# Out-projections from three fp32r terms, row statistics by column half, and a diagonal matrix in place of a scaled copy

## The chip, the cores and the metric

One Trainium2 core runs the whole forward pass as one program. The metric is the time of one execution on the device in microseconds, lower is better; it is given as the median of several runs. The engines are TensorE (PE, matmuls into PSUM), VectorE (DVE), ScalarE (ACT), GpSimd (POOL) and SyncE (SP, whose queue issues nearly all weight transfers here). Each engine takes its instructions in the order of the program and waits for the others by semaphores.

## The reference, cut to what matters

The input is 256 tokens by 1024 columns (and a second stream of 256 context tokens). Three attention blocks follow each other, each closed by an out-projection, a residual and a mixture of experts:

```python
# phase A: one block with two streams; then layers l = 0 and l = 1
h   = rms_norm(x, g1) (modulated in phase A)
p   = h @ w_in                      # 1024 x IN_WIDTH
mix = concat of the heads' outputs  # 256 x 1024, 8 slots of 128 columns
x   = x + mix @ w_out               # 1024 x 1024, the out-projection
h2  = rms_norm(x, g2)
x   = x + moe(h2)                   # 32 experts in 4 groups, top 2, hidden 512
...
out = rms_norm(x, g_final)          # after phase A's and the last block's experts
```

All weights and values are float32, and `mix @ w_out` and the norms have to be as good as float32.

## The kernel before, in words

**Weights.** Weights stream from memory in units of 1 MB (128 partitions x 2048 floats) into a ring of slots, 23 that rotate and 14 lent out for work space early in the program. `S.take()` gives the next unit in the order of the program, `S.borrow()` takes a slot for a work buffer, and `S.release()` gives slots back; the SP queue issues the units strictly in that order, each as soon as its slot is free. So a slot that is released late delays every unit behind it.

**Precision.** A matmul can take fp32 or fp32r (a shortened fp32). Where the weights are split, each operand is written as hi + lo, with hi a copy to fp32r and lo the difference, and `mm3` (line 561) makes three fp32r matmuls: hi·hi, hi·lo and lo·hi. The in-projections do that already: ACT copies (L821, L1950), DVE or POOL subtracts (L822, L1954). The out-projections take plain fp32 (`out_mm`, L596): per 128 rows and 512 columns 8 matmuls of fp32, which the trace records as 2 instructions each.

**Attention slots.** `run_items` (L762) is a software pipeline written by hand: in slot s the scores of item s, the softmax of an earlier item, its transposes (L2160), their copies (`pT`, L2162), the value matmuls (L2125, L2129), and then a filler from a string. In layers 0 and 1 the twelve items are `MMSSMMSSMMMM`; for an M item the softmax is L2144 (DVE), L2148 (DVE), L2149 (ACT), L2153 and L2154 (DVE) and L2155 (POOL scales one of its parts). The fillers hold the out-projection: `o` opens it, `o2` does its first two slots of `mix`, and so on to `o8`, all for rows 0 to 127 and columns 0 to 511. Phase A has a string of its own, with L1339, L1347 to L1354, L1290 and L1293 as one slot's score, softmax, transposes and copy.

**Out-projection and routing.** `out_route` does the other groups of the out-projection, `group(0, 512)`, `group(1, 0)`, `group(1, 512)` and `group(1, 768)`, adds the residual, and chooses the experts (`choose`, L703 one of its DVE steps; `split`, L726 and L727). Then the gather (L1520) and the expert matmuls (L1704) start.

**Experts.** The expert matmuls are fed by 1 MB units. The last block's results are scattered to rows (L1762) and added to X (L1893, L1895).

**Statistics and norm.** After the experts, ACT squares the new rows (L1873) and sums them; `inv_root` takes the inverse root by row half `a`. In `normB` DVE writes a scaled copy of X (L1967), TensorE transposes it in 16 pieces of 128x128 (L1976), and ACT and DVE write it as hi and lo (L1980, L1982). Only then can the in-projection start (L2001). In layer 0, POOL scales X itself (L1970).

Of the kernel before, what the change touches and what calls it, by code (L numbers as in the profile page):

```python
# [10 lines left out]
F32 = mybir.dt.float32  # L11
# [13 lines left out]
FILL_B = ". v0 v1 . u0 . . u1 p0 f p1 f+o o2 o4+o5 o6"  # L25
# [3 lines left out]
FILL_A = "k0 . k1 . . q . r1 va+vb+m1 m1 . m6+r2+rel sl sb . o+o4 o6 o7 ."  # L29
# [343 lines left out]
def hybrid_kernel(ctx: ExitStack, tc: tile.TileContext, A, out, dbg=None):  # L373
# [211 lines left out]
    def out_begin(ps, mixT, order):  # L585
        O = K()
        O.mixT, O.order, O.n = mixT, order, 0
        O.us = [S.take() for _ in range(4)]
        O.w = [u.t.rearrange("p (f c) -> p f c", f=4) for u in O.us]
        O.po = bank(ps, "tr")  # L590
        return O
# [11 lines left out]
    def out_route(kind, O, E, finish, wr, brow, xT, tmp, spent):  # L603
# [129 lines left out]
        S.release(*O.us[0:2])  # L733
# [8 lines left out]
        S.release(*O.us[2:4])  # L742
# [36 lines left out]
    def first_phase():  # L779
        with ExitStack() as es:  # L780
# [446 lines left out]
            mixT = b2.t.rearrange("p (a d) -> p a d", a=8)  # L1227
            r = inv_rms(wg, p, 64, [128, 512], "_")
# [20 lines left out]
            def values(h, dT, vals, w, kind):  # L1249
                hp, odd = h // 2, h % 2  # L1250
                if kind == "n":
# [8 lines left out]
                    act.activation(mixT[:, 6 + hp], po[:, 0:256], AF.Copy)  # L1260
# [12 lines left out]
                def norm():  # L1273
                    pq = bank(ps, "tr")
                    pe.matmul(pq, lhsT=ones, rhs=sq, start=True, stop=True)
                    r = inv_rms(wd, pq, 128, [128, 512], "_")
                    later.append(lambda: dve.scalar_tensor_tensor(
                        mixT[:, 2 * hp:2 * hp + 2].rearrange("p a t -> p (a t)"), po, gs, r, op0=OP.mult, op1=OP.mult))
                later.append(norm)

# [114 lines left out]

            def start_out():
                hold.O = out_begin(ps, mixT, range(8))
# [14 lines left out]
            def last_b():  # L1412
                last[1]()
                S.release(*lent[:8])
# [3 lines left out]
            jobs.update({f"o{n}": lambda n=n: out_part(hold.O, n) for n in range(1, 9)})  # L1418
            jobs.update({f"m{n}": lambda n=n: [mod_unit(mod2) for _ in range(n)] for n in range(1, 9)})
# [15 lines left out]
            def finish(a, sl, po):  # L1435
# [4 lines left out]
                             ([], [b2]))  # L1440

    def moe_phase(kind, l, R, final=None):
# [7 lines left out]
        with ExitStack() as es:  # L1450
# [283 lines left out]

            def down(p, src):
                s = st[p]
                s.y = []
                for hf in range(2):
                    pd = mm()
                    for f in range(nf):  # L1740
                        pair_mm(pd, lambda a, b: s.hT[:, f, a:b], src.down(p, f, hf), f == 0, f == nf - 1)
                        if hf == 1 and f == nf // 2:
                            scat(p, [(0, 0), (1, 0)])
                    end = p == NL - 1 and hf == 1
                    yh = wk.tile([128, 512], F32R, name="P" if end else "yh")
                    yl = wk.tile([128, 512], F32R, name="xg" if end else "yl")
                    if kind == 1:
                        dve.scalar_tensor_tensor(pd, pd, s.gt, gmod[:, hf * 512:(hf + 1) * 512], op0=OP.mult,  # L1748
                                                 op1=OP.mult)
                        act.activation(yh, pd, AF.Copy)  # L1750
                        dve.tensor_sub(yl, pd, yh.bitcast(F32))
                    else:
                        act.activation(yh, pd, AF.Copy, scale=s.gt)  # L1753
                        dve.scalar_tensor_tensor(yl, pd, s.gt, yh.bitcast(F32), op0=OP.mult, op1=OP.subtract)  # L1754
                    s.y.append((yh, yl))
# [107 lines left out]
            vrt = [[[cons.tile([128, 1], F32, name=f"f{c}{a}{i}") for c in "vrt"] for i in range(nv)] for a in range(2)]  # L1863

            def stats():
                junk = {}

                def square(a, i, hf, on_act):
                    v, o = y[2 * a + hf] if i == 0 else blk(X.t, a, hf), ss[:, a, i, hf:hf + 1]
                    if on_act not in junk:  # L1870
                        junk[on_act] = mm()
                    if on_act:
                        act.activation(junk[on_act], v, AF.Square, scale=1.0 / 32, accum_out=o)  # L1873
                    else:
                        dve.scalar_tensor_tensor(junk[on_act], v, 1.0 / 1024, v, op0=OP.mult, op1=OP.mult, accum_out=o)

                def total(a):
                    for i in range(nv):
                        v = vrt[a][i][0]
                        if i == 0:  # L1880
                            dve.scalar_tensor_tensor(v, ss[:, a, 0, 0:1], EPS, ss[:, a, 0, 1:2], op0=OP.add, op1=OP.add)
                        else:
                            dve.tensor_add(v, ss[:, a, 1, 0:1], ss[:, a, 1, 1:2])
# [407 lines left out]
```

## Time and profile before

| | us |
|---|---|
| median of 3 runs | 1371.52 (1367.01 to 1372.51) |
| profiled execution, its own time | 1366.64 |
| its span in the trace | 1364.5 |
| PE busy / DVE / ACT / POOL | 1202.4 / 428.9 / 340.0 / 92.7 |
| mean granted clock of TensorE | 0.956 of full speed |

The span is what the trace covers; 2.1 us lie around it. A busy PE is not a PE at its peak. The profile's slices show the transfers at their full rate in the expert stages and at rest for part of each attention stage.

### The profile page before, as it was taken

What the parts mean: (1) busy time and instruction counts of PE and PEld (TensorE: products, weight loads), DVE (VectorE), ACT (ScalarE), POOL (GpSimd) and SP (SyncE); (2) the same over time, 40 slices, a digit from 0 to 9 for tenths busy, and PEclk for the clock granted to TensorE, in tenths of its full rate; (3) what the DMA queues carried; (4) which work ended last, traced back from release to release, by engine and by line L of the source; (5) the groups of instructions that cost most, each with busy time, mean ns of one, the idle gap of its engine ahead of it and who ended that gap; (6) DMA issues with size and microseconds to landing.
All of it is one profiled execution on the core that took longest, in us unless ns stands there. A gap on an engine that the chain in (4) does not pass through costs nothing. (4 is left out here: it accounts for less than half of the span.)

```text
span 1364.5 us, 18768 instructions
## 1 busy us (share of the span) xinstructions
PE 1202.4 (88%) x7278; PEld 649.5 (48%) x7278; DVE 428.9 (31%) x1022; ACT 340.0 (25%) x706; POOL 92.7 (7%) x79
## 2 busy tenths in 40 slices
PE   5999999999976799999769998999768999999775
PEld 3788765554221144443248664543216856444221
DVE  5456453342101021221155434221105535322102
ACT  4432343221000010110145521211014642212102
POOL 1344100000000000000012100000000210000000
PEclk9999998999989899999879998998898999999988
DMA  9644508959999999999993547999999365899995
GB/s 370 249 183 174 212 32 329 379 217 397 421 421 421 421 421 421 420 418 421 420 421 143 221 193 322 422 421 420 421 420 419 137 278 215 360 420 421 421 421 222
DMA packets 64537, 459.40 MB, mean 337 GB/s; under 512 B 7409, under 2 KB 7729, under 8 KB 9905
## 3 DMA queue, kind: packets, MB, share of 16 engines
q1 hardware_dynamic: 64432, 458.04, 82.0%
q8 instruction: 62, 1.02, 0.3%
q14 instruction: 43, 0.34, 0.1%
HBM read 466.40 MB, written 1.05 MB: 343 GB/s over the span
## 5 line engine op out<-in xcount | busy, mean ns | idle before, releaser
L1704 PE MATMUL up<-ring,xg 128*32 128x512 f32 (+2 forms) x2016 | 366.0, 629 | 52.9 <-DMA ring<-in_gu_dram 29.5
L1704 PEld LDWEIGHTS up<-ring,xg 128*32 128x32 f32 (+2 forms) x2016 | 103.6, 125 | 284.0 <-issue 180.5
L1704 PE MATMUL mm<-ring,hdT 128*32 128x512 f32 (+2 forms) x1008 | 194.3, 634 | 35.1 <-DMA ring<-in_dn_dram 23.8
L561 PE MATMUL ps<-ring,ring 128*128 128x256 f32 (+1 forms) x960 | 143.3, 307 | 1.2 <-POOL ring L896 0.5
L561 PEld LDWEIGHTS ps<-ring,ring 128*128 128x128 f32 x960 | 128.2, 192 | 20.4 <-issue 5.2
L1720 DVE TENSOR_TENSOR hd<-hd,up 128x256 f32<-128x256 f32 (+1 forms) x32 | 16.7, 521 | 352.1 <-ACT hd L1719 332.5
L1704 PEld LDWEIGHTS mm<-ring,hdT 128*32 128x32 f32 (+2 forms) x1008 | 52.2, 125 | 149.8 <-issue 99.2
L1719 ACT ACTIVATE hd<-up 128x256 f32<-128x256 f32 (+1 forms) x32 | 14.9, 465 | 364.9 <-PE up L1704 364.9
L1520 PEld LDWEIGHTS mm<-P,ring 128*128 128x128 f32 x512 | 66.2, 199 | 12.2 <-issue 8.8
L1520 PE MATMUL mm<-P,ring 128*128 128x256 f32 x512 | 70.4, 294 | 0.7 <-DVE xg L1530 0.3
L596 PE MATMUL mm<-ring,ring 128*128 128x512 f32 (+1 forms) x192 | 64.1, 487 | 0.0
L1754 DVE SCALAR_TENSOR_TENSOR yl<-mm,gt,yh 128x512 fp32r<-128x512 f32 x38 | 28.5, 751 | 113.2 <-ACT yh L1753 113.2
L1748 DVE SCALAR_TENSOR_TENSOR mm<-mm,gt,gmod 128x512 f32<-128x512 f32 x24 | 18.2, 759 | 111.3 <-PE mm L1704 111.3
L1753 ACT ACTIVATE yh<-mm,gt 128x512 fp32r<-128x512 f32 x38 | 26.1, 687 | 108.1 <-PE mm L1704 73.0
L1750 ACT ACTIVATE yh<-mm 128x512 fp32r<-128x512 f32 x23 | 13.7, 597 | 143.3 <-DVE mm L1748 143.3
L2001 PE MATMUL ps<-ring,ring 128*128 128x256 f32 x384 | 49.3, 290 | 0.0
L2001 PEld LDWEIGHTS ps<-ring,ring 128*128 128x128 f32 x384 | 48.2, 197 | 0.2
L596 PEld LDWEIGHTS mm<-ring,ring 128*128 128x128 f32 x192 | 35.8, 190 | 23.7 <-issue 21.5
L1970 POOL TENSOR_SCALAR ring<-ring,fr 128x1024 f32<-128x1024 f32 x2 | 5.7, 2848 | 421.5 <-DMA ring<-in_win_dram 421.5
L822 POOL TENSOR_TENSOR ring<-ring,ring 128x1024 fp32r<-128x1024 f32 x12 | 29.9, 2490 | 56.4 <-ACT ring L821 49.3
L1954 DVE TENSOR_TENSOR ring<-ring,ring 128x1024 fp32r<-128x1024 f32 x24 | 28.1, 1222 | 14.6 <-ACT ring L1950 14.6
L1762 PE MATMUL po<-yh,sm 128*128 128x512 f32 x61 | 30.6, 502 | 1.7 <-ACT yh L1750 1.0
(459 smaller groups left out, 1340.1 us busy)
## 6 DMA issues: line engine op xcount, KB each, us to landing
ring<-in_gu_dram SPq DMA_DIRECT2D x128, 1024.0 KB, 19.7
ring<-in_dn_dram SPq DMA_DIRECT2D x124, 1024.0 KB, 19.7
ring<-in_up_dram SPq DMA_DIRECT2D x120, 1024.0 KB, 19.5
ring<-in_wmod_dram SPq DMA_DIRECT2D x24, 1024.0 KB, 6.9
ring<-in_win_dram SPq DMA_DIRECT2D x24, 1024.0 KB, 11.4
ring<-in_wout_dram SPq DMA_DIRECT2D x12, 1024.0 KB, 18.3
ring<-in_c_dram SPq DMA_DIRECT2D x2, 896.0 KB, 14.2
ring<-in_wsm_dram SPq DMA_DIRECT2D x2, 784.0 KB, 14.9
```

Of the source, the lines that this page charges most:

```text
L561: pe.matmul(out, lhsT=a, rhs=b, start=first and i == 0, stop=last and i == 2, skip_group_check=True)
L596: pe.matmul(po, lhsT=O.mixT[:, s, a * 128:(a + 1) * 128], rhs=O.w[2 * c + s // 4][:, s % 4, sl.start - 512 * c:sl.stop - 512 * c], start=( ...
L822: (pool if q else dve).tensor_sub(lo[:, sl], u.t[:, sl], hi[:, sl].bitcast(F32))
L1520: pe.matmul(o, lhsT=xx[:, a, dt * 128:(dt + 1) * 128], rhs=P[:, a], start=(k == 0), stop=(k == 3))
L1704: pe.matmul(out[w * e:w * e + w], lhsT=x_of(w * e, w * e + w), rhs=wt, start=start, stop=stop)
L1720: dve.tensor_mul(hd, hd, pu[:, hid:uw])
L1748: dve.scalar_tensor_tensor(pd, pd, s.gt, gmod[:, hf * 512:(hf + 1) * 512], op0=OP.mult, op1=OP.mult)
L1753: act.activation(yh, pd, AF.Copy, scale=s.gt)
L1754: dve.scalar_tensor_tensor(yl, pd, s.gt, yh.bitcast(F32), op0=OP.mult, op1=OP.subtract)
L1762: pe.matmul(y[2 * a + hf], lhsT=s.sm[:, a * 128:(a + 1) * 128], rhs=s.y[hf][i], start=False, stop=True, skip_group_check=True)
L1954: dve.tensor_sub(lo[:, sl], u.t[:, sl], hi[:, sl])
L2001: pe.matmul(p[:, f * 256:(f + 1) * 256], lhsT=w[pw][:, dt, f * 128:(f + 1) * 128], rhs=hT[ph][:, dt], start=(i == 0 and f == 0 and dt == 0 ...
```

## The change

Three things are changed together.

First, the out-projection takes `mm3` in place of fp32. Four new fillers, `w0` to `w3`, one for each unit of `w_out`, copy the unit to hi on ACT in two halves (L590 of the changed kernel) and subtract the first half on DVE and the second on POOL (L591). `mix` is stored as hi and lo as well (ACT and DVE; in phase A partly POOL). The hi and lo parts hold eight slots where the four units were, and `mix` two where it held one; they take over six work slots that were released earlier (`hu`, `hl`, `sets`), and are released after `group(1, 0)` and `group(1, 768)`. `normB` reserves 6 slots where it reserved 5.

Second, the statistics after the experts go by column half instead of row half, with DVE's keep and ACT's square on different halves, one inverse root for all four values, and, in the last expert block, matmuls of the two column halves interleaved by pairs of units.

Third, `normB` writes no scaled copy: DVE makes two diagonal matrices (the identity times the row scales), and TensorE multiplies X's pieces by them in fp32, which transposes and scales at once. POOL's scaling of X stands behind them.

```diff
-FILL_B = ". v0 v1 . u0 . . u1 p0 f p1 f+o o2 o4+o5 o6"
+FILL_B = ". v0 v1 . u0 . . u1 p0+w0 f+w1 p1+w2 f+w3+o o2 o4+o5 o6"
-FILL_A = "k0 . k1 . . q . r1 va+vb+m1 m1 . m6+r2+rel sl sb . o+o4 o6 o7 ."
+FILL_A = "k0 . k1 . . q . r1 va+vb+m1 m1 . m6+r2+rel sl+w0 sb+w1 w2 w3+o+o4 o6 o7 ."
...
+    def out_weights(O, hi, lo=None):
+        u, i = S.take(), len(O.us)
+        lo = lo or S.borrow(F32R)
+        for q in range(2):
+            sl = slice(q * 1024, (q + 1) * 1024)
+            act.activation(hi.t[:, sl], u.t[:, sl], AF.Copy)
+            (pool if q else dve).tensor_sub(lo.t[:, sl], u.t[:, sl], hi.t[:, sl].bitcast(F32))
+        if i < 2:
+            S.reserve(1)
+        S.release(u)
+        O.us.append((hi, lo))
...
-            pe.matmul(po, lhsT=O.mixT[:, s, a * 128:(a + 1) * 128],
-                      rhs=O.w[2 * c + s // 4][:, s % 4, sl.start - 512 * c:sl.stop - 512 * c], start=(k == 0), stop=(k == 7))
+            mm3(po, lambda z: O.w[2 * c + s // 4][z][:, s % 4, sl.start - 512 * c:sl.stop - 512 * c],
+                lambda z: O.mix[z][:, s, a * 128:(a + 1) * 128], k == 0, k == 7, flip=True)
...
         group(1, 0, 512, 2)
-        S.release(*O.us[0:2])
+        S.release(*O.us[0], *O.us[1])
...
         group(1, 768, 256, 4)
-        S.release(*O.us[2:4])
+        S.release(*O.us[2], *O.us[3])
...
+            square(0, 0, 0, True)
+            keep(1, 0)
+            square(1, 0, 0, True)
+            keep(0, 0)
+            square(0, 0, 1, True)
+            keep(1, 1)
+            square(1, 0, 1, True)
+            keep(0, 1)
...
+            inv_root(wx, v, 2 * nv, "", (r, t))
...
-            S.reserve(5)
+            S.reserve(6)
...
-            for hf in range(2):
-                for a in range(2):
-                    dve.tensor_scalar(blk(xn, a, hf), blk(X.t, a, hf), R.vrt[a][-1][1], None, op0=OP.mult)
...
+            for a in range(2):
+                dve.tensor_scalar(dg[:, a], ident, R.vrt[a][-1], None, op0=OP.mult)
...
-                        pe.transpose(pt[:, i * 256 + a * 128:i * 256 + (a + 1) * 128],
-                                     xn[:, a, (2 * dp + i) * 128:(2 * dp + i + 1) * 128], ident)
+                        pe.matmul(pt[:, i * 256 + a * 128:i * 256 + (a + 1) * 128],
+                                  lhsT=X.t[:, a, (2 * dp + i) * 128:(2 * dp + i + 1) * 128], rhs=dg[:, a], start=True,
+                                  stop=True)
...
-            mu = S.borrow()
+            mixu = [S.borrow(F32R) for _ in range(2)]
...
+            def store(i, src, **kw):
+                act.activation(mix[0][:, i], src, AF.Copy, **kw)
...
+                    dve.tensor_sub(mix[1][:, i], src, mix[0][:, i].bitcast(F32))
...
-                    S.release(hu, hl, *sets[0], *sets[1])
...
+            jobs.update({f"w{n}": lambda n=n: out_weights(O, sets[n // 2][n % 2], (hu, hl)[n] if n < 2 else None) for n in range(4)})
```

How instructions move shows on two engines in the attention slots of layer 0. The first is GpSimd, from the set-up of the items to the routing; `e` are an item's exponentials, L2155 scales them, and L727 is the routing's split. Before:

```order
L2096 COPY wsm<-ring_1793 128x256
L2098 TENSOR_TENSOR wrk<-ring_1793,vecs 128x288
L2155 TENSOR_SCALAR e<-e,sm 128x128 x8
L727 TENSOR_TENSOR ring_6383<-ring_5615,ring_6382 128x1024
L1825 TENSOR_LOAD info
```

And the same place after, where L2155 is L2200 and L727 is L741:

```order
L2132 COPY wsm<-ring_2292 128x256
L2134 TENSOR_TENSOR wrk<-ring_2292,vecs 128x288
L2200 TENSOR_SCALAR e<-e,sm 128x128 x4
L591 TENSOR_TENSOR ring_2090<-ring_2179,ring_5712 128x1024
L591 TENSOR_TENSOR ring_5711<-ring_2181,ring_5713 128x1024
L2200 TENSOR_SCALAR e<-e,sm 128x128
L591 TENSOR_TENSOR ring_6392<-ring_112,ring_5714 128x1024
L2200 TENSOR_SCALAR e<-e,sm 128x128
L591 TENSOR_TENSOR ring_6422<-ring_72,ring_5715 128x1024
L2200 TENSOR_SCALAR e<-e,sm 128x128 x2
L741 TENSOR_TENSOR ring_6496<-ring_5697,ring_6495 128x1024
```

Two subtractions of 128x1024 now stand ahead of the ninth item's scaling (item 8, counting M and S items from 0), one ahead of item 9's and one ahead of item 10's.

The second is ScalarE in the same slots; L2149 are the exponentials of an item, two rows each, L2162 the copies `pT`, L2220 a copy for the filler `p0` or `p1`, and L2131 stores `mix`. Before:

```order
L2220 ACTIVATE dT<-tr 128x256
L2149 ACTIVATE e,sm<-e,nm 128x256
L2149 ACTIVATE e,sm<-e,nm 128x128
L2201 ACTIVATE zm<-zm 128x384
L2225 ACTIVATE ring_77<-tr,vecs 128x256
L2149 ACTIVATE e,sm<-e,nm 128x256
L2149 ACTIVATE e,sm<-e,nm 128x128
L2131 ACTIVATE ring_77<-po 128x256
L2162 ACTIVATE pT<-tr 128x384
L2220 ACTIVATE dT<-tr 128x256
L2149 ACTIVATE e,sm<-e,nm 128x256
```

After, with L2265 for L2220, L2194 for L2149, L2207 for L2162, L2246 for L2201 and L2152 for the stores:

```order
L2265 ACTIVATE dT<-tr 128x256
L590 ACTIVATE ring_5712<-ring_2179 128x1024 x2
L2194 ACTIVATE e,sm<-e,nm 128x256
L2194 ACTIVATE e,sm<-e,nm 128x128
L2246 ACTIVATE zm<-zm 128x384
L2152 ACTIVATE ring_6048<-tr,vecs 128x256
L590 ACTIVATE ring_5713<-ring_2181 128x1024 x2
L2194 ACTIVATE e,sm<-e,nm 128x256
L2194 ACTIVATE e,sm<-e,nm 128x128
L2152 ACTIVATE ring_6048<-po 128x256
L2207 ACTIVATE pT<-tr 128x384
L2265 ACTIVATE dT<-tr 128x256
```

Each `w` filler's two copies stand at the end of their slot, ahead of the next slot's exponentials; the third and the fourth stand behind a `pT`, which waits for GpSimd's scaling of an item.

## Rows read from the trace of the kernel before

**Rows 1.** The page's second part: transfer rate in 40 equal slices of the span.

```profile
GB/s 370 249 183 174 212 32 329 379 217 397 421 421 421 421 421 421 420 418 421 420 421 143 221 193 322 422 421 420 421 420 419 137 278 215 360 420 421 421 421 222
```

**Rows 2.** Windows of two stages: stretch, length, engines' busy times, clock, DMA share, GB/s.

```profile
721.00:790.00 69.00, 64.91 (x413) 50.98 (x412) 33.95 (x73) 38.53 (x92) 12.52 (x14) 1.00 0.48 190
...
840.00:1050.00 210.00, 181.70 (x1178) 79.80 (x1171) 48.72 (x101) 43.73 (x86) 0.00 (x0) 0.94 1.01 421
```

**Rows 3.** The chain that ended last, 830 to 1032: start, us, what.

```profile
1004.87 20.77 DMA ring<-in_dn_dram
1025.68 3.62 PE mm L1704 x26
```

**Rows 4.** Timeline, SP queue, 736 to 860: start, length, unit transfers issued.

```profile
813.53 21.84 SPq L332 DMA_DIRECT2D ring<-in_dn_dram  x8
840.35 9.55 SPq L332 DMA_DIRECT2D ring<-in_gu_dram  x8
```

**Rows 5.** Timeline, PE: layer 0's out-projection groups and the first gather.

```profile
789.28 7.03 PE L596 MATMUL mm<-ring,ring 128*128 128x512 f32 x16
...
809.88 3.62 PE L596 MATMUL mm<-ring,ring 128*128 128x256 f32 x16
...
823.86 6.34 PE L1520 MATMUL mm<-P,ring 128*128 128x256 f32 x32
```

**Rows 6.** Timeline, PE: runs of 24 fp32r matmuls (`mm3` of 8), two widths.

```profile
89.22 5.73 PE L561 MATMUL ps<-ring,ring 128*128 128x512 f32 x24
...
764.32 3.12 PE L561 MATMUL ps<-ring,ring 128*128 128x256 f32 x24
```

**Rows 7.** Line groups, splits of other weights: duration in ns min/median/max.

```profile
L821 ACT ACTIVATE ring<-ring x24: 1041/1048/1064, 24.4 to 184.6; 128x1024 fp32r<-128x1024 f32 x24
L822 DVE TENSOR_TENSOR ring<-ring,ring x12: 1214/1224/1730, 25.5 to 184.8; 128x1024 fp32r<-128x1024 f32 x12
L822 POOL TENSOR_TENSOR ring<-ring,ring x12: 2392/2420/2857, 26.4 to 185.8; 128x1024 fp32r<-128x1024 f32 x12
```

**Rows 8.** Timeline, layer 0's slots 8 to 11.

```profile
771.03 0.37 ACT L2220 ACTIVATE dT<-tr 128x256 f32<-128x256 f32 x1
...
773.66 0.66 POOL L2155 TENSOR_SCALAR e<-e,sm 128x128 f32<-128x128 f32 x1 [9.70 <-PE ps L2139]
...
779.87 0.66 POOL L2155 TENSOR_SCALAR e<-e,sm 128x128 f32<-128x128 f32 x1 [0.35 <-DVE sm L2153]
```

**Rows 9.** Timeline, layer 0's routing: a DVE and a POOL operation side by side.

```profile
818.94 2.34 POOL L727 TENSOR_TENSOR ring<-ring,ring 128x1024 fp32r<-128x1024 f32 x1 [38.41 <-DVE o L702]
818.96 2.37 DVE L703 TENSOR_TENSOR o<-o,rg 128x32 f32<-128x32 f32 x1
```

**Rows 10.** Timeline, phase A: DVE's first softmax step of two slots.

```profile
235.23 0.42 DVE L1347 TENSOR_TENSOR pe<-ps,ring 128x256 f32<-128x256 f32 x1 [1.51 <-PE ps L1339]
239.38 0.42 DVE L1347 TENSOR_TENSOR pe<-ps,ring 128x256 f32<-128x256 f32 x1 [2.00 <-PE tr L1290]
```

**Rows 11.** Timeline, from the last scatters of phase A's experts to layer 0's norm.

```profile
690.87 0.50 PE L1762 MATMUL po<-yh,sm 128*128 128x512 f32 x1
...
692.00 1.06 PE L1704 MATMUL mm<-ring,hdT 128*32 128x512 f32 x8
...
694.01 0.60 ACT L1750 ACTIVATE P<-mm 128x512 fp32r<-128x512 f32 x1 [4.13 <-DVE mm L1748]
...
696.74 0.58 ACT L1873 ACTIVATE mm<-po 128x512 f32<-128x512 f32 x1
...
703.40 1.66 DVE L1967 TENSOR_SCALAR ring<-ring,fr 128x512 f32<-128x512 f32 x4
...
704.03 3.77 PE L1976 MATMUL ps<-cm,ring 128*128 128x128 f32 x16 [7.48 <-DVE ring L1967]
```

**Rows 12.** A window there; columns as in Rows 2.

```profile
704.00:708.00 4.00, 3.97 (x18) 3.85 (x19) 2.89 (x8) 3.15 (x8) 3.05 (x2) 0.50 1.02 421
```

**Rows 13.** Timeline, PE: one fp32 matmul of 128x128, two records.

```profile
760.91 0.38 PE L2198 MATMUL tr<-sp,ones 128*128 128x128 f32 x2
```

More of the change, by code (lines that the diff above doesn't have):

```diff
@@ L583, in banks, with out_new, out_begin @@
         return E
-    def out_begin(ps, mixT, order):
+    def out_weights(O, hi, lo=None):
[9 more added lines that the diff above has]
+        O.us.append((hi, lo))
+        O.w.append([v.t.rearrange("p (f c) -> p f c", f=4) for v in (hi, lo)])
+    def out_new(mix, order):
         O = K()
-        O.mixT, O.order, O.n = mixT, order, 0
-        O.us = [S.take() for _ in range(4)]
-        O.w = [u.t.rearrange("p (f c) -> p f c", f=4) for u in O.us]
+        O.mix, O.order, O.n = mix, order, 0
+        O.us, O.w = [], []
+        return O
+    def out_begin(O, ps):
         O.po = bank(ps, "tr")
-        return O
     def out_mm(O, po, a, sl, ks):
@@ L1733, in tr, with split_y @@
                 dve.tensor_scalar(s.sm, iota, gt[:, p % 2, 0:1], None, op0=OP.is_equal)
+            def split_y(p, hf, pd):
+                s = st[p]
+                end = p == NL - 1 and hf == 1
+                yh = wk.tile([128, 512], F32R, name="P" if end else "yh")
+                yl = wk.tile([128, 512], F32R, name="xg" if end else "yl")
+                if kind == 1:
+                    dve.scalar_tensor_tensor(pd, pd, s.gt, gmod[:, hf * 512:(hf + 1) * 512], op0=OP.mult, op1=OP.mult)
+                    act.activation(yh, pd, AF.Copy)
+                    dve.tensor_sub(yl, pd, yh.bitcast(F32))
+                else:
+                    act.activation(yh, pd, AF.Copy, scale=s.gt)
+                    dve.scalar_tensor_tensor(yl, pd, s.gt, yh.bitcast(F32), op0=OP.mult, op1=OP.subtract)
+                s.y[hf] = (yh, yl)
@@ L1735, in down @@
             def down(p, src):
                 s = st[p]
-                s.y = []
-                for hf in range(2):
[L1739 to L1755, printed above, removed]
@@ new lines, in down @@
+                s.y, pds = {}, {}
+                last = p == NL - 1
+                m = 2 if last else nf
+                for z in range(0, nf, m):
+                    for hf in range(2):
+                        if z == 0:
+                            pds[hf] = mm()
+                        for f in range(z, z + m):
+                            pair_mm(pds[hf], lambda a, b: s.hT[:, f, a:b], src.down(p, f, hf), f == 0, f == nf - 1)
+                            if hf == 1 and f == (nf - 1 if last else nf // 2):
+                                scat(p, ALL[0:2])
+                        if z + m == nf:
+                            split_y(p, hf, pds[hf])
@@ L1907, in moe_phase, with square @@
-            stats()
+            v, r, t = (cons.tile([128, 2, nv], F32, name=f"f{c}{nv}") for c in "vrt")
+            junk = {}
+            def square(a, i, hf, on_act):
+                x, o = y[2 * a + hf] if i == 0 else blk(X.t, a, hf), ss[:, a, i, hf:hf + 1]
+                if on_act not in junk:
+                    junk[on_act] = mm()
+                if on_act:
+                    act.activation(junk[on_act], x, AF.Square, scale=1.0 / 32, accum_out=o)
+                else:
+                    dve.scalar_tensor_tensor(junk[on_act], x, 1.0 / 1024, x, op0=OP.mult, op1=OP.mult, accum_out=o)
@@ L1908, in moe_phase @@
+            dve.scalar_tensor_tensor(v[:, :, 0:1], ss[:, :, 0, 0:1], EPS, ss[:, :, 0, 1:2], op0=OP.add, op1=OP.add)
+            if nv == 2:
+                dve.tensor_add(v[:, :, 1:2], ss[:, :, 1, 0:1], ss[:, :, 1, 1:2])
+                dve.scalar_tensor_tensor(v[:, :, 1:2], v[:, :, 0:1], EPS, v[:, :, 1:2], op0=OP.mult, op1=OP.add)
+            inv_root(wx, v, 2 * nv, "", (r, t))
+            vrt = [[r[:, a, i:i + 1] for i in range(nv)] for a in range(2)]
             if final is not None:
@@ L1933, in second_phase @@
             mark("normB")
[L1934 removed]
+            dg = lu.t[:, 1024:1280].rearrange("p (a t) -> p a t", a=2)
             hold = Unit()
@@ L1984, in second_phase @@
             low()
+            if l == 0:
+                for a in range(2):
+                    pool.tensor_scalar(X.t[:, a], X.t[:, a], R.vrt[a][0], None, op0=OP.mult)
             mark("inprojB")
@@ L2130, in pv @@
                               start=False, stop=True)
-                act.activation(mixT[:, slot + hp], po[:, 0:256], AF.Copy)
+                store(slot + hp, po[:, 0:256])
             def mla_item(h):
```

100 lines of the change are left out of this document (44 added, 56 removed).

## The prediction

> **What bounds the kernel now.** I read the transfer rates first [rows 1]. From slice 10 on the expert stages run at 418 to 422 GB/s, and the two attention stages between them fall to between 137 and 360. A 1 MB unit at 421 GB/s takes 2.49 us. The window of layer 0's experts shows the transfers busy all the time (share 1.01) and TensorE 181.7 of 210 us, while the window of its attention slots shows them 0.48 busy [rows 2]. The chain agrees: at the end of the experts it runs through the landings of the last units, and then a few matmuls [rows 3]. So an expert stage ends when its units have come, and an attention stage when its own chain of small steps has. What starts the stream again is the expert stage's first matmuls: the ring is full by then, SP's last eight issues before it are spread over 21.84 us, and the next eight come at 840.35, once slots come free [rows 4]. Therefore a shift of the end of the attention stage goes one to one into the end of the experts behind it, and so do slots that come free late. A gain on TensorE inside an expert stage would be worth nothing; a gain or a loss between the last landing and the first gather counts in full.
>
> **The out-projection groups.** A group of 512 columns takes 7.03 us in 16 records of fp32, one of 256 columns 3.62 [rows 5]. The same eight steps as 24 fp32r matmuls take 5.73 and 3.12 [rows 6]. So two groups save 1.30 and two 0.50: 3.6 us behind the slots, and 1.3 more for the group that is done inside the slots, which counts only if TensorE is what the slots wait for.
>
> **The weight splits.** The trace has the same splits for other weights: 1.05 us for an ACT copy of half a unit, 1.22 for DVE's subtraction, 2.42 for POOL's [rows 7]. One out-projection adds 8, 4 and 4 of these: 8.4, 4.9 and 9.7 us. The engines have room for them by sum, since DVE was busy 33.95, ACT 38.53 and POOL 12.52 of 69 us [rows 2]. But the slots are chains, and the order shows where the splits stand in them: two POOL subtractions ahead of item 8's scaling, one ahead of item 9's and one ahead of item 10's; and on ACT each pair of copies ahead of the next exponentials, the third and fourth pair behind a `pT` that waits for such a scaling.
>
> I follow layer 0 on the clock of before [rows 8]. `dT` ends at 771.40, the copies of `w0` at 773.5, DVE's part at about 774.6 (behind a step of its own), POOL's at 777.0. DVE's next step on the S item reads two buffers, and if it has to wait for POOL, the next exponentials come at 779.6 and end the copies of `w1` at 782.6; POOL is done at 785.0 and scales item 8 by 785.7. Before, that was done at 774.3. From there each slot is a ring of steps: transposes, `pT` and one more ACT store, about 1.45 together (three steps of the size of `dT`'s 0.37, with 0.1 each to hand over), two copies 2.1, POOL's subtraction 2.4, the scaling 0.66, in all 6.6 us. That gives 792.3 and 798.9 for items 9 and 10, and 799.6 for item 11, where 780.5 was before. From there to the end of the group in the slots it was 8.8 us (789.28); I take 6.2, since fewer of its matmuls are left and they are cheaper. The slots then end at about 806, 16.5 later.
>
> Whether DVE waits for POOL is the main unknown. In the routing a DVE step of 128x32 took 2.37 us, next to a POOL step of 2.34 that began 0.02 earlier [rows 9]; a subtraction of 128x1024 takes DVE only 1.22 [rows 7]. I read that as a lock on operations with two buffers as input. Without the lock the slots end 2.4 us earlier, at +14. The page SBUF — State Buffer of the Trainium skill (section on the two physically separate sides) states such a lock: VectorE and GpSimd share a pair of ports, and whichever starts first holds it for its whole instruction. By that rule the slots come out at +16.5, and without it at +14; the trace's 2.37 us agrees with the rule.
>
> I take +16, less 3.6 for the groups: +12.4 at the first gather (823.86 before [rows 5]). The ring adds a little: ten slots come free only with the groups, four behind `group(1, 0)` and six behind `group(1, 768)`, where five did before. Five more units at 2.49 us are 12.5 us of transfers which lay in idle time before and now start after about 825; the stream goes on without a gap from there, and its first units of the second round land 13 us later than before. I take 12.5 per layer, bounds +8 (ACT's copies find half their place in waits) and +16 (no overlap at all): **+25 for both layers**.
>
> **Phase A.** Its slots have the same four fillers, with two full sections of DVE and ACT ahead of the softmax: 1.05 + 1.22 = 2.27 us each, 9.1 for four. DVE's first softmax step waited 1.51 and 2.00 us for TensorE in two of the slots [rows 10]; so 3.5 are hidden and 5.6 remain, less 3.6 for the groups: **+2**. Bounds: -5 if all is hidden, +5.5 if nothing is.
>
> **Statistics and norm.** In phase A's last block the scatter of four matmuls stands ahead of the last eight matmuls (690.87 to 692.00, then 1.06 us), and now stands behind them; with the pairs interleaved, some 16 matmuls fewer are left behind the last landing. That brings `P` (694.01) forward by 1.1 + 1.5 = 2.6 us [rows 11]. Behind it the old way takes 9.4 us until 703.40; the new one has six squares on ACT of 0.58 and a read of the sum each [rows 11], overlapping the last scatter, and one root instead of two, so I expect the scale near 699.1 and TensorE's start near 699.5, 4.5 earlier than 704.03. Then it pays: the 16 transposes took 3.77 us, one record each, and an fp32 matmul of 128x128 is two records [rows 13]. At the clock that these transposes ran at, 0.50 of full speed [rows 12], the 1.2 GHz level, 16 more records cost 3.4 us; at 2.4 GHz the whole stage would be as long as it is now. I take half of that: **-3**, bounds -4.6 and -1. In layer 1 the statistics gain only 0.8, since nothing is interleaved there and only one root falls away, and the matmuls lose between 0 and 3.4: **+1**. The tail after the last experts has one root for two and no norm: 0.
>
> TensorE was idle for 7.48 us ahead of the transposes [rows 11], and the clock stayed at 0.50 for the first 4 us of transposes although TensorE was 3.97 of 4.00 us busy [rows 12]. The page TensorE: Matmul & The Clock Gate of the Trainium skill (Part 4, PE-mode transpose) says that the full clock does not engage for transposes. By that rule matmuls in their place could raise the clock early, and the two norms would be worth -4.5 and -1 in place of -3 and +1; no row here tells that from a clock that would have risen anyway.
>
> **The sum.** +25 + 2 - 3 + 1 = +25 on the profiled 1366.6, so **1391**; that execution is 4.9 us below the median of the runs shown, and I keep to it.
>
> **The rivals.** (1) *The splits are hidden* in the idle time of the three engines. Then each out-projection saves 4.9 us, three save 14.7, with 2 for the norms: about 1350. For it: the busy sums [rows 2]. Against it: four slots of such a chain have no more than a microsecond or two of slack each. It decides the sign where a split lengthens a slot by less than 0.9 us, since four slots times 0.9 are the 3.6 of the groups. (2) *Only ACT's copies count*, POOL's subtractions run beside the slots: four slots grow by 1.2 us, 4.8 less 3.6 is +1.2 per layer; with +1 in phase A and -2 in the norms, about 1368, no change. Against it: the scaling stands behind the subtraction in GpSimd's order. (3) *More is lost than the chain*: with long waits in the slots the clock falls to 1.2 GHz. It stood at 1.00 of full speed through the slots before [rows 2]; half speed through one group and the last slots costs 5 us per layer, and a gap of the same kind in phase A 3: about 1404.
>
> **How the numbers follow.** Forecast (1382 to 1398) 0.60; hidden 0.17; no change 0.10; more lost 0.13. A measurement of this kernel can tell about 0.5%, 7 us, from no change, so faster 0.17, same 0.10, slower 0.73. The range goes from 1363, below the no-change case, to 1404; it leaves out most of the hidden case and the end of the third.
>
> **What would show it.** In the changed profile: the four scalings of items 8 to 11 end near 786, 792, 799 and 800 on before's clock (slots of about 6.6 us); the out-projection groups at 5.7 and 3.1 us; DVE steps with two buffers as input stretched to POOL's end; the first gather 12 us later in each layer, counted from the end of the phase before; the norm's first matmul about 4.5 us earlier in layer 0; transfers at 421 GB/s to the end of each expert stage. The forecast is wrong if the slots stay near 4 us, if POOL's 2.4 us lie behind something longer, or if the late start of the experts is caught up because their units had already landed.

## The result, and the profile after

The changed kernel takes 1410.72 us (median, 1409.86 to 1410.94) where the kernel before takes 1369.26 (1366.26 to 1372.51) on the same chip: the ratio is 1.0308, with a 95% interval from 1.029 to 1.0326. The profiled execution has a span of 1408.2 us, 43.7 more than before. So the sign was as forecast, and the loss was 41 us where 25 were forecast, outside the range.

First the page's slices of the transfer rate, which answer to [rows 1]:

```profile
GB/s 368 256 175 203 151 31 269 327 355 422 421 421 421 421 421 421 421 420 421 419 232 90 80 292 421 421 421 421 421 419 276 91 78 298 419 421 420 421 421 226
```

The expert stages still run at 419 to 422; the valleys of the two layers are deeper, 80 and 78 where 143 and 137 were the lowest. Where the time went is read from stage to stage. This table has the start of certain instructions on TensorE's timeline of both kernels: the first gather of each expert stage, the last scatter, the first score of a layer.

| | before | after | shift | grown by |
|---|---|---|---|---|
| first gather, phase A | 285.71 | 288.90 | +3.2 | +3.2 |
| first score, layer 0 | 742.62 | 742.10 | -0.5 | -3.7 |
| first gather, layer 0 | 823.86 | 844.05 | +20.2 | **+20.7** |
| last scatter, layer 0 | 1031.43 | 1052.14 | +20.7 | +0.5 |
| first score, layer 1 | 1074.58 | 1096.12 | +21.5 | +0.8 |
| first gather, layer 1 | 1155.28 | 1195.47 | +40.2 | **+18.7** |
| last scatter, layer 1 | 1354.82 | 1398.81 | +44.0 | +3.8 |

Nearly all of it lies in the two layers' attention slots. The out-projection groups behind them did what was worked out: the timeline of TensorE, for [rows 5], has

```profile
813.37 5.62 PE L561 MATMUL mm<-ring,ring 128*128 128x512 f32 x24
...
830.52 3.12 PE L561 MATMUL mm<-ring,ring 128*128 128x256 f32 x24
...
844.05 6.13 PE L1556 MATMUL mm<-P,ring 128*128 128x256 f32 x32
```

5.62 and 3.12 us for 7.03 and 3.62. The splits cost what their rows said too; the line groups (duration in ns, minimum, median, maximum) for [rows 7]:

```profile
L590 ACT ACTIVATE ring<-ring x24: 1042/1046/1054, 233.0 to 1152.5; 128x1024 fp32r<-128x1024 f32 x24
...
L591 DVE TENSOR_TENSOR ring<-ring,ring x12: 1224/1225/1226, 234.1 to 1152.7; 128x1024 fp32r<-128x1024 f32 x12
L591 POOL TENSOR_TENSOR ring<-ring,ring x12: 2374/2431/2471, 235.1 to 1153.7; 128x1024 fp32r<-128x1024 f32 x12
```

What the slots did with them is in the timeline of layer 0 (start, us, engine, line, tiles; in brackets the idle time before and who ended it), from GpSimd's part of the first split on, with one row from ahead of it. L2237 is a step of an S item with two buffers as input, L2194 are the exponentials, L2199 and L2200 the scaling on VectorE and GpSimd, L2189 and L2193 the next item's first softmax steps:

```profile
764.98 0.35 DVE L2199 TENSOR_SCALAR e<-e,sm 128x256 f32<-128x256 f32 x1
...
777.68 2.43 POOL L591 TENSOR_TENSOR ring<-ring,ring 128x1024 fp32r<-128x1024 f32 x1 [11.87 <-ACT ring L590]
777.83 2.69 DVE L2237 SCALAR_TENSOR_TENSOR sp<-zm,sp 128x384 f32<-128x384 f32 x1
...
781.54 0.51 ACT L2194 ACTIVATE e<-e,nm 128x256 f32<-128x256 f32 x1 [3.94 <-DVE nm L2193]
...
784.12 1.99 ACT L590 ACTIVATE ring<-ring 128x1024 fp32r<-128x1024 f32 x2
...
785.20 1.22 DVE L591 TENSOR_TENSOR ring<-ring,ring 128x1024 fp32r<-128x1024 f32 x1 [0.46 <-ACT ring L590]
786.19 2.43 POOL L591 TENSOR_TENSOR ring<-ring,ring 128x1024 fp32r<-128x1024 f32 x1 [6.08 <-ACT ring L590]
...
786.54 2.24 DVE L2199 TENSOR_SCALAR e<-e,sm 128x256 f32<-128x256 f32 x1
788.61 0.64 POOL L2200 TENSOR_SCALAR e<-e,sm 128x128 f32<-128x128 f32 x1
788.70 0.54 DVE L2189 TENSOR_TENSOR e<-ps,ring 128x384 f32<-128x384 f32 x1
789.27 0.61 DVE L2193 TENSOR_REDUCE nm<-e 128x1 f32<-128x256 f32 x2
...
789.79 0.51 ACT L2194 ACTIVATE e<-e,nm 128x256 f32<-128x256 f32 x1 [3.67 <-DVE nm L2193]
...
797.75 0.51 ACT L2194 ACTIVATE e<-e,nm 128x256 f32<-128x256 f32 x1 [3.75 <-DVE nm L2193]
```

The reader is to see a ring. ACT copies, then DVE and POOL subtract, then DVE scales (2.24 us, where the same step alone takes 0.35, the first row), then DVE starts the next item's softmax, and only then ACT has its exponentials and can go on to the next copies. Only pieces of this overlap: DVE's subtraction runs beside the second copy, and DVE's scaling beside POOL's subtraction, with which it ends (788.78 and 788.62). The next item's softmax and exponentials run beside none of it. In the kernel before, these are the exponentials of the same slots:

```profile
769.39 0.51 ACT L2149 ACTIVATE e<-e,nm 128x256 f32<-128x256 f32 x1 [2.12 <-DVE nm L2148]
...
772.84 0.51 ACT L2149 ACTIVATE e<-e,nm 128x256 f32<-128x256 f32 x1 [1.44 <-DVE nm L2148]
...
774.87 0.51 ACT L2149 ACTIVATE e<-e,nm 128x256 f32<-128x256 f32 x1 [0.28 <-DVE nm L2148]
...
778.50 0.51 ACT L2149 ACTIVATE e<-e,nm 128x256 f32<-128x256 f32 x1 [1.63 <-DVE nm L2148]
```

They come 2.0 to 3.6 us apart; in the changed kernel 8.25 and 7.96.

### The profile page after: what moved, and what is told of

Read it like the earlier page. It is cut to its first block, busy times and chain, and to the rows that moved or that the text cites. A ratio compares the mean times of both kernels' runs of the same rounds, so it can differ in the third digit from the quotient of the medians.

```text
span 1408.2 us, 19149 instructions
## 1 busy us (share of the span) xinstructions
PE 1211.5 (86%) x7430; PEld 677.7 (48%) x7430; DVE 463.8 (33%) x1031; ACT 363.4 (26%) x723; POOL 126.6 (9%) x94
## 2 busy tenths in 40 slices
DMA packets 64540, 459.44 MB, mean 326 GB/s; under 512 B 7408, under 2 KB 7728, under 8 KB 9904
## 5 line engine op out<-in xcount | busy, mean ns | idle before, releaser
L1740 PE MATMUL up<-ring,xg 128*32 128x512 f32 (+2 forms) x2016 | 371.5, 640 | 54.8 <-DMA ring<-in_gu_dram 30.9
L561 PE MATMUL mm<-ring,ring 128*128 128x256 f32 (+1 forms) x288 | 52.8, 339 | 0.0
L561 PEld LDWEIGHTS mm<-ring,ring 128*128 128x128 f32 x288 | 44.4, 190 | 5.6
L836 POOL TENSOR_TENSOR ring<-ring,ring 128x1024 fp32r<-128x1024 f32 x12 | 29.9, 2494 | 56.3 <-ACT ring L835 49.3
L591 POOL TENSOR_TENSOR ring<-ring,ring 128x1024 fp32r<-128x1024 f32 x12 | 29.1, 2428 | 60.7 <-ACT ring L590 42.6
L2205 PE MATMUL tr<-cm,e 128*128 128x128 f32 x48 | 10.3, 333 | 27.4 <-POOL e L2200 27.4
```

Source lines behind the costliest of these rows:

```text
L561: pe.matmul(out, lhsT=a, rhs=b, start=first and i == 0, stop=last and i == 2, skip_group_check=True)
L591: (pool if q else dve).tensor_sub(lo.t[:, sl], u.t[:, sl], hi.t[:, sl].bitcast(F32))
L836: (pool if q else dve).tensor_sub(lo[:, sl], u.t[:, sl], hi[:, sl].bitcast(F32))
L1740: pe.matmul(out[w * e:w * e + w], lhsT=x_of(w * e, w * e + w), rhs=wt, start=start, stop=stop)
```

## The experiments

The distance from a layer's first score to its first gather is named *slots and groups* below; it is 81.2 and 80.7 us before (layers 0 and 1), 102.0 and 99.4 after. Each run was timed together with the kernel before. Where totals of two runs are compared, each is taken by its *loss*, its median less that of the kernel before beside it; the changed kernel's loss is 41.5 us.

**The parts alone.** `e1_norm_only` has the second and third part of the change and fp32 out-projections, `e2_proj_only` the first part alone, `e3_stats_only` the statistics and the interleaved last block alone. The edit of the third, seen from `e1_norm_only`:

```diff
-            for a in range(2):
-                dve.tensor_scalar(dg[:, a], ident, R.vrt[a][-1], None, op0=OP.mult)
+            for hf in range(2):
+                for a in range(2):
+                    dve.tensor_scalar(blk(xn, a, hf), blk(X.t, a, hf), R.vrt[a][-1], None, op0=OP.mult)
...
-                        pe.matmul(pt[:, ...], lhsT=X.t[:, a, ...], rhs=dg[:, a], start=True, stop=True)
+                        pe.transpose(pt[:, ...], xn[:, a, ...], ident)
```

> The kernel before with the second and third part of the change (statistics by column half, diagonal matrix) and the out-projections left as fp32. Theory (the loss is all in the attention slots of the out-projection's weight splits): faster than before by 2 to 4 us, from -3.8 in layer 0's norm and +1.1 in layer 1's, as the trace of the change has them, and -2.6 from the interleaved last block. Rival (the diagonal matrix or the statistics bring part of the loss): slower than before by 2 us or more.

> The kernel before with the first part alone: three-term out-projections with weight splits, and statistics and transposes as before. Theory: all of the loss and a little more, 1412 to 1416 us, with layer slots as long as in the changed kernel (24 us longer than before). Rival (the parts hurt each other, for example by the reserved slots or by the clock after the norm): clearly less, 1395 to 1405 us.

> The kernel before with the statistics by column half and the interleaved last block alone; the scaled copy and the transposes stay. Theory: faster than before by 4 to 6 us (4.5 in layer 0, 0.8 in layer 1), and so 1 to 3 us faster than the run with the diagonal matrix, since 16 more records on TensorE at half clock are not paid. Rival by the clock (real matmuls raise TensorE's clock, transposes do not): slower than the run with the diagonal matrix by 2 us.

Measured: 1365.94 us, ratio 0.9971 (0.9958 to 0.9983); 1416.23 us, ratio 1.0341 (1.0321 to 1.0361); and 1361.52 us, ratio 0.9946 (0.9929 to 0.9962), against 1369.45 of the kernel before. So the loss is the first part's, all of it, and the statistics alone are 7.9 us faster than the kernel before, more than the 4 to 6 expected. The diagonal matrix costs 4.4 us of that. In layer 0 the timelines of TensorE of the run with the diagonal matrix and of the one without show the stage itself:

```profile
698.85 5.74 PE L1972 MATMUL ps<-ring,ring 128*128 128x128 f32 x32 [5.54 <-DVE ring L1966]
```

```profile
698.50 3.77 PE L1976 MATMUL ps<-cm,ring 128*128 128x128 f32 x16 [5.74 <-DVE ring L1967]
```

32 records in 5.74 us for 16 in 3.77. The rival by the clock has something in it: these are windows of the two runs (stretch, length, busy times, granted clock, DMA), with the matmuls first,

```profile
700.00:702.00 2.00, 2.00 (x12) 2.00 (x11) 0.20 (x1) 0.84 (x2) 0.00 (x0) 0.50 1.01 422
702.00:704.00 2.00, 2.00 (x16) 2.00 (x16) 1.17 (x4) 1.04 (x3) 0.00 (x0) 0.77 1.02 413
704.00:706.00 2.00, 2.00 (x17) 1.77 (x16) 1.72 (x5) 2.00 (x5) 1.45 (x1) 1.00 1.00 418
```

and then the transposes:

```profile
700.00:702.00 2.00, 2.00 (x12) 2.00 (x10) 1.39 (x4) 1.91 (x6) 2.00 (x1) 0.50 1.03 430
702.00:704.00 2.00, 2.00 (x12) 2.00 (x11) 1.96 (x6) 2.00 (x5) 2.00 (x2) 0.50 0.99 406
704.00:706.00 2.00, 2.00 (x18) 2.00 (x18) 2.00 (x3) 1.03 (x2) 1.09 (x1) 0.95 1.04 431
```

With matmuls TensorE leaves its 1.2 GHz level about 1.3 us earlier: 0.77 and 0.95 are means of 0.50 and 1.00 over 2 us, which puts the rise at about 702.9 and 704.2. But that gains less than the 16 records cost: the in-projection starts at 704.35 in the one and at 701.92 in the other.

**The held ring slots.** `e7_hold` is the kernel before with the six work slots released behind the last group:

```diff
-                    S.release(hu, hl, *sets[0], *sets[1])
...
-            return out_route(2, hold.O, E, finish, wrk, brow[:, 1 + l], lu.t, lu.t, ([mu], [lu]))
+            return out_route(2, hold.O, E, finish, wrk, brow[:, 1 + l], lu.t, lu.t, ([mu, hu, hl, *sets[0], *sets[1]], [lu]))
```

> The kernel before, with the six work slots hu, hl and sets of layers 0 and 1 released only behind group(1, 768), as the change does, and nothing else. Theory (the held slots cost little as long as the slots' chain is what is late): the attention slots and the first gather stay as before, and the first units of the experts' second round land later, 0 to 14 us in all. Rival (the held slots are the main part of the loss): 25 us slower or more.

Measured: 1384.00 us, ratio 1.011 (1.0091 to 1.013), 14.5 us slower. The slots and groups stay as they were, 81.3 and 80.9. The time is lost behind them: from the first gather to the last scatter layer 0 takes 215.8 us for 207.6, layer 1 208.3 for 199.5. That is just above what the theory allowed (0 to 14), and not the main part of the loss. But the run holds more than the change does: it gives back two slots behind `group(1, 0)` and nine behind `group(1, 768)`; the changed kernel gives back four and six there, and the four raw units of `w_out` earlier, at the splits. So its 14.5 us are not the price of the change's held slots. In the changed kernel the same distances are 208.1 and 203.3, and in `e10_copies_only` below, which holds what the change holds, with slots and groups 1.5 and 5.0 us longer than before, they are 209.0 and 203.3: 1.5 and 3.7 us more than before.

**Which engine subtracts, and what stands behind it.** Three variants of the changed kernel. `e4_split_dve` has both subtractions on VectorE, `e5_scale_dve` moves L2200 from GpSimd to VectorE, `e6_store_late` writes the low part of each stored item of `mix` one slot later:

```diff
-            (pool if q else dve).tensor_sub(lo.t[:, sl], u.t[:, sl], hi.t[:, sl].bitcast(F32))
+            dve.tensor_sub(lo.t[:, sl], u.t[:, sl], hi.t[:, sl].bitcast(F32))
```

```diff
-                    pool.tensor_scalar(e[:, 256:384], e[:, 256:384], sm[:, 1:2], None, op0=OP.mult)
+                    dve.tensor_scalar(e[:, 256:384], e[:, 256:384], sm[:, 1:2], None, op0=OP.mult)
```

```diff
             def store(i, src, **kw):
+                settle()
                 act.activation(mix[0][:, i], src, AF.Copy, **kw)
...
-                    dve.tensor_sub(mix[1][:, i], src, mix[0][:, i].bitcast(F32))
+                    pend.append(lambda: dve.tensor_sub(mix[1][:, i], src, mix[0][:, i].bitcast(F32)))
...
```

`settle()` makes the subtractions that are pending.

> The changed kernel with both halves of each weight split's subtraction on VectorE, none on GpSimd. Theory (VectorE is held while GpSimd subtracts, and the scaling of the items stands behind it; VectorE then needs 1.22 us where it waited 2.4): each of the four slots shorter by 0.9 to 1.5 us, 4 to 6 us per layer, 1399 to 1404 us in all. Rival (VectorE becomes the bound, or the slots wait for ACT's copies alone): within 3 us of the changed kernel's 1410.7.

> The changed kernel with the third part of each M item's scaling moved from GpSimd to VectorE, so that nothing of the items stands behind a weight split in GpSimd's queue; the splits stay where they are. Theory by the lock (VectorE's own scaling waits for GpSimd's subtraction anyway): 0 to 4 us faster than the changed kernel. Rival by order (it is GpSimd's queue that makes the slots long): four times 2.4 us per layer, 15 to 20 us faster, 1391 to 1396 us.

> The changed kernel with the low part of each stored item of mix subtracted one slot later, so that VectorE's next reciprocal does not stand behind a subtraction that waits for ACT's store. Theory (this wait cost 3.9 us in layer 0 and 2.4 us in layer 1 ahead of the first split): 4 to 7 us faster than the changed kernel, 1404 to 1407 us. Rival (the splits' chain absorbs it): within 2 us.

Measured, against 1368.37 of the kernel before: 1412.63 us, 1.0325 (1.0304 to 1.0346); 1415.43 us, 1.0334 (1.0304 to 1.0365); 1407.32 us, 1.0287 (1.0267 to 1.0308). Slots and groups: 100.1 and 97.7; 103.3 and 100.9; 97.9 and 98.0. So GpSimd's queue is not the cause: with nothing of the items behind its subtractions the slots are no shorter (the rival by order falls). And with no subtraction on GpSimd at all, 1.8 and 1.6 us per layer come back, less than the 4 to 6 expected; phase A, where VectorE was busier, gave more than that away (its first gather at 294.42; runs with the changed kernel's own phase A have it from 288.63 to 291.26). VectorE's scaling takes 0.35 again, but the ring has the same order, with 2.36 us of subtraction on VectorE in it, and its turn is 7.5 us:

```profile
789.01 0.51 ACT L2194 ACTIVATE e<-e,nm 128x256 f32<-128x256 f32 x1 [2.93 <-DVE nm L2193]
...
792.67 2.36 DVE L591 TENSOR_TENSOR ring<-ring,ring 128x1024 fp32r<-128x1024 f32 x2 [0.46 <-ACT ring L590]
...
795.14 0.35 DVE L2199 TENSOR_SCALAR e<-e,sm 128x256 f32<-128x256 f32 x1
...
796.51 0.51 ACT L2194 ACTIVATE e<-e,nm 128x256 f32<-128x256 f32 x1 [2.92 <-DVE nm L2193]
```

The late store gave back 4.1 us in layer 0 and 1.3 in layer 1; its loss is 39.0 for 41.5, so 2.5 us in the whole, less than the 4 to 7 expected. In the changed kernel VectorE's reciprocal stood behind the subtraction of `mix`, which waited 1.97 us for ACT's store; TensorE then idled 2.35 us, and the next projection ran slower. First the changed kernel's timeline, then that of the late store:

```profile
764.45 0.42 DVE L2157 TENSOR_TENSOR ring<-po,ring 128x256 fp32r<-128x256 f32 x1 [1.97 <-ACT ring L2152]
764.79 0.15 DVE L2198 RECIPROCAL sm<-sm 128x2 f32<-128x2 f32 x1
...
765.86 0.55 PE L2205 MATMUL tr<-cm,e 128*128 128x128 f32 x3 [2.35 <-POOL e L2200]
766.17 4.60 PE L561 MATMUL ps<-ring,ring 128*128 128x256 f32 x24
```

```profile
764.55 3.11 PE L561 MATMUL ps<-ring,ring 128*128 128x256 f32 x24
```

**The subtractions left out.** `e9_copies_only` dropped them and let the third term read the high part of `w_out` with the high part of `mix`. That doubles the main term of the out-projection, and with it the values by which the experts are chosen.

> The changed kernel without the subtractions of the weight splits: only ACT's copies stay, and the matmuls of the low part read the high part in its place, so the output lacks the low part of w_out. Theory (of the 24 us that the slots grew by, GpSimd's subtractions and what waits for them are 2.4 to 2.7 us in each of four slots): 18 to 22 us faster than the changed kernel, 1389 to 1393 us; then the late release of the ring's slots, 14.5 us by itself, is the larger part of what is left. Rival (ACT's copies make the slots long): 8 us faster or less.

It took 1426.47 us, ratio 1.043 (1.0376 to 1.0483), with other transfers (446.89 MB for the changed kernel's 459.44), so its time says nothing on the slots. The slots and groups themselves, 82.9 and 85.9 us, agree with the next run. `e10_copies_only` has the third term read the high part of `w_out` with the low part of `mix`, which keeps the sizes:

```diff
-            (pool if q else dve).tensor_sub(lo.t[:, sl], u.t[:, sl], hi.t[:, sl].bitcast(F32))
...
+            for i, z in enumerate((0, 1, 1)):
+                pe.matmul(po, lhsT=O.mix[z][:, s, a * 128:(a + 1) * 128],
+                          rhs=O.w[2 * c + s // 4][0][:, s % 4, sl.start - 512 * c:sl.stop - 512 * c],
...
```

> The changed kernel without the subtractions of the weight splits: only ACT's copies stay, and the out-projection's third term takes the high part of w_out with the low part of mix, so that as many matmuls run, and the low part of w_out is left out. Theory (exponentials and scalings wait for the subtractions, whichever engine makes them: in the changed trace the next exponentials start 3.6 us after the second copy ends): from the first score of a layer to its first gather 88 to 92 us, where the changed kernel took 102.0 and 99.4 and the one before 81.2 and 80.7; 1390 to 1398 us in all, since the held ring slots then become what is late. Rival (ACT's copies make the slots long): 96 us or more from score to gather.

Measured: 1374.54 us, ratio 1.0039 (1.0022 to 1.0055): a loss of 6.1 us for 41.5, so 35 us are gone, more than expected. Slots and groups take 82.8 and 85.7 us, shorter than either theory had it, with all of ACT's copies, `mix` in two parts and the held slots still there. The next item's softmax steps (L2190, L2194) run beside the copies, and the exponentials follow the copies at once:

```profile
774.75 0.49 ACT L2195 ACTIVATE e<-e,nm 128x256 f32<-128x256 f32 x1
...
776.39 2.00 ACT L590 ACTIVATE ring<-ring 128x1024 fp32r<-128x1024 f32 x2
...
777.38 0.55 DVE L2190 TENSOR_TENSOR e<-ps,ring 128x384 f32<-128x384 f32 x1
777.97 0.61 DVE L2194 TENSOR_REDUCE nm<-e 128x1 f32<-128x256 f32 x2
...
778.48 0.51 ACT L2195 ACTIVATE e<-e,nm 128x256 f32<-128x256 f32 x1
...
782.17 0.50 ACT L2195 ACTIVATE e<-e,nm 128x256 f32<-128x256 f32 x1
```

They are 3.7 us apart. So 2.4 us of subtraction make a slot 4.3 us longer: without it VectorE does the next item's first steps while ACT copies, with it they stand behind it.

**The clock.** `e11_warm` puts eight matmuls that nobody reads behind each split, in TensorE's idle time:

```diff
+                p = bank(ps)
+                for i in range(8):
+                    pe.matmul(p[:, 0:128], lhsT=ones, rhs=ident, start=True, stop=True)
```

> The changed kernel with 8 more fp32 matmuls of 128x128 behind each of the four splits of layers 0 and 1, in TensorE's idle time; their result is not read. Theory (TensorE's clock, 0.61 to 0.79 of full speed in these slots, stretches the matmuls on the path): the clock rises in the slots, and from score to gather it is 2 to 4 us shorter per layer, 1403 to 1407 us. Rival (the clock costs little, since the slots wait for ACT, DVE and POOL): within 1 us per layer, or longer by what the added matmuls take.

Measured: 1408.27 us, ratio 1.0292 (1.0265 to 1.0318). The granted clock from 774 to 805 rises from 0.71 and 0.61 of full speed (two windows) to 0.89 and 0.77; the second of these, in the changed kernel and then here:

```profile
790.00:805.00 15.00, 7.14 (x28) 4.76 (x28) 9.81 (x14) 7.61 (x18) 6.40 (x5) 0.61 0.24 75
```

```profile
790.00:805.00 15.00, 10.81 (x60) 9.47 (x60) 10.31 (x15) 7.79 (x18) 6.21 (x5) 0.77 0.20 71
```

Slots and groups take 101.6 and 98.0, 0.4 and 1.3 less, not the 2 to 4 of this run's theory. So as far as the clock was raised, it is worth about 1 us per layer; that rival of the prediction is not the cause.

**The same work in another order.** `e12_sub_late` writes each subtraction one slot later, behind the next item's first softmax steps (`split_low` makes those of the split before), and `e13_both_late` adds the late store of `mix`:

```diff
+        split_low(O)
         u, i = S.take(), len(O.us)
...
             act.activation(hi.t[:, sl], u.t[:, sl], AF.Copy)
-            (pool if q else dve).tensor_sub(lo.t[:, sl], u.t[:, sl], hi.t[:, sl].bitcast(F32))
...
+        O.late.append((u, hi, lo, i))
...
```

> The changed kernel with each weight split's subtractions written one slot later: the copies stay where they are, and the subtractions of w0 come behind the next slot's first softmax steps, just ahead of the copies of w1, and so on. The work is the same. Theory (the loss is the order: ACT's copies, the subtraction and VectorE's first softmax steps of the next item follow each other in a ring instead of running side by side): the exponentials come every 4 to 5 us in place of 8, and from the first score to the first gather it is 86 to 92 us per layer, 102.0 and 99.4 in the changed kernel; 1380 to 1392 us in all. Rival (the work itself is too much for the slots, wherever it stands): 97 us or more per layer.

> The run before it together with the low part of mix stored one slot later. Theory (two separate waits): a further 2 to 5 us in all. Rival (one hides the other): the same within 1.5 us. Either way it stays above the kernel before, since the ring slots that are held cost 14.5 us by themselves as soon as the slots' chain no longer covers them.

Measured, against 1367.41 of the kernel before: 1388.07 us, 1.0146 (1.012 to 1.0172), and 1383.83 us, 1.01 (1.0064 to 1.0136). Slots and groups are 90.6 and 89.1, then 86.6 and 86.6. The exponentials come 5.1 and 4.4 us apart:

```profile
780.62 0.50 ACT L2203 ACTIVATE e<-e,nm 128x256 f32<-128x256 f32 x1
...
785.72 0.51 ACT L2203 ACTIVATE e<-e,nm 128x256 f32<-128x256 f32 x1 [1.46 <-DVE nm L2202]
...
790.09 0.51 ACT L2203 ACTIVATE e<-e,nm 128x256 f32<-128x256 f32 x1 [0.58 <-DVE nm L2202]
```

The work is the changed kernel's, instruction for instruction; only the order is another, and half of the loss is gone: 20.7 us for 41.5, and 16.4 with the late store too. Both theories' numbers held here, but for the first of the two distances (5.1 for 4 to 5). Both kernels stay above the one before, and not for the held slots in the main, as was expected of the second: its slots and groups are still 5.4 and 5.9 us longer than before, its expert stages, from first gather to last scatter, 0.9 and 2.8.

## Why the prediction was right and wrong

**Right:** that the loss is in the layers' slots, that a VectorE step with two buffers as input waits for GpSimd (L2237 took 2.69 us beside the first subtraction, and 0.55 alone), and that the loss goes one to one to the end (the experts behind them add 0.5 us in layer 0, as the ring was said to, and 3.8 in layer 1, which is more). The groups (3.6 us) and the durations of the splits were as taken. Phase A: +3.2 at its first gather, 1.2 of which was there before its first split at 233.0 (an in-projection ahead of it starts at 200.81 for 199.65), for +2. The norms: -3.7 and +0.8 for -3 and +1.

**Wrong:** the term of the slots, +16 per layer before the groups' gain. It measured 20.7 + 3.6 = 24.3 and 18.7 + 3.6 = 22.3. Three steps of it were too small. First, the ring of a slot, "in all 6.6 us": I had it run through GpSimd's subtraction, the item's scaling, its transposes and `pT`. It runs through VectorE: the scaling there waits for GpSimd too, and the next item's two softmax steps (0.54 and 0.61 us) and the exponentials stand behind that. From one item's scaling on GpSimd to the next, as the prediction counts, a turn took 7.93 and 7.34 us (788.61, 796.54, 803.88): 2.1 too little over the two turns. I had taken the lock from a step with two buffers as input and not counted it for one with a single buffer. Second, the cost of storing `mix` as two parts ahead of the first split was put at nothing. The score of the item ahead of that split starts at 770.61 for 767.28, and item 8's scaling ends at 789.25, which is 789.8 on before's clock, 4.1 us behind the forecast 785.7. With the late store it ends 42.6 us behind the layer's first score, where the forecast had 43.1, and slots and groups got 4.1 and 1.3 us shorter. Third, the end, from the last scaling to the end of the group: 8.1 us for 6.2. Together that is 8.1 of the 8.3 us that layer 0 lost beyond the forecast; the 6.3 us of layer 1 were not divided in this way.

The cause that I gave first, GpSimd's order and lock, is only a small part: without either, 1.8 us per layer come back. What the runs show in its place is the serial order of copy, subtraction and next softmax, whichever engine subtracts; leaving the subtraction out gives 35 us, writing it one slot later 20.8. Of the remaining 9.4 us of slots and groups in layer 0 (90.6 against 81.2, and 3.6 more with the groups' gain) the late store takes 4.0; how the rest divides between ACT's copies, VectorE's time and the lock was not tried.

Of the rivals, the hidden splits are what the changed order moves towards, but even `e10_copies_only` stays 6 us above the kernel before: its slots and groups are 1.5 and 5.0 us longer in spite of the groups' gain of 3.6, and its expert stages 1.5 and 3.7. So the copies, with `mix` in two parts, cost 5.1 and 8.6 us per layer, where the second rival had 4.8 for the copies alone. The third rival's time, 1404, is the nearest to the measured one, but by luck: the clock did fall, but raising it gave back about 1 us per layer, and the rival had 5.

## What to carry to other kernels

Idle sums of the engines say nothing on whether new work fits into a hand-written pipeline: look for where in each engine's order it stands, and whether the next item's first step stands behind it. A split that is written one slot later costs the same work and, here, 20.8 us less. Buffers that a faster matmul needs can be paid in the stream that feeds what comes next. Holding the buffers alone prices that only if they come free in the same steps as in the change: nine slots behind the last group cost 14.5 us in `e7_hold`, while the expert stages of the run with the change's own steps grew by 5.2.

## What was not expected of the hardware

- A VectorE operation with one SBUF input and a scalar also waits for GpSimd: L2199, 128x256, takes 0.35 us alone and 2.24 beside GpSimd's subtraction of 128x1024, and ends when that does. Of the Trainium skill the page SBUF — State Buffer (the section on the two physically separate sides) has it so for VectorE's operations in a 2-port mode as well as for those with two SBUF inputs. These runs agree with their 0.35 and 2.24 us, though no row shows the mode that L2199 ran in; the prediction had counted only the operations with two inputs.
- It goes both ways: in `e12_sub_late` one GpSimd subtraction of 128x1024, begun 0.02 us behind a VectorE subtraction of the same size, took 3.44 us for the usual 2.36:

```profile
794.38 1.22 DVE L601 TENSOR_TENSOR ring<-ring,ring 128x1024 fp32r<-128x1024 f32 x1
794.40 3.44 POOL L601 TENSOR_TENSOR ring<-ring,ring 128x1024 fp32r<-128x1024 f32 x1
```

- TensorE's clock left the 1.2 GHz level about 1.3 us earlier with 32 records of matmuls than with 16 transposes at the same place, so the page TensorE: Matmul & The Clock Gate of the Trainium skill (Part 4, PE-mode transpose) is borne out in direction; the time that it gave back was less than the 16 records cost.
